# Hymba layer on one core: parts of queries and keys in turn by rows, three transfers a head, values in four groups

## The chip, the core and the metric

The kernel runs on one core of one Trainium2 chip. Its engines are TensorE (PE in the profile; its weight loads are PEld), VectorE (DVE), ScalarE (ACT), GpSimd (POOL) and SyncE (SP), which here only issues transfers; ScalarE issues some too. The metric is device time in microseconds. Three runs of the kernel before took 2397.44, 2400.09 and 2403.56 us; the median is 2400.09.

## What is computed

One decoder layer on 2048 tokens of width 1024, in float32. The part that matters here is mixer B, the dilated attention: 8 heads of 64 channels, each in three branches with (window, dilation) of (128, 1), (512, 4) and (2048, 16). In each branch the keys are gathered by stride, a query sees at most 129 of them, and a bias row by distance is added. The three outputs are then weighted by their softmax denominators:

```python
for window, dilation in DSA_PATTERN:
    o, lse = dilated_branch(q, k, v, rel_bias, window, dilation)
    outs.append(o); lses.append(lse)
w = jax.nn.softmax(jnp.stack(lses, axis=0), axis=0)
return jnp.sum(w[..., None] * jnp.stack(outs, axis=0), axis=0)
```

Ahead of it stands one projection of the normed input (`w_in`), beside it mixer A (chunked gated linear attention, GLA), and behind both the output projection, a squared-ReLU MLP and the last norm.

## The kernel before, in words

The kernel has three stages, one after the other: the projection (to about 553 us), the attention with GLA woven in (to about 955 us), and output projection and MLP. Products in float32 are made of parts: a value is split into `hi`, a rounded copy, and `lo`, the rest.

*Projection.* `finish` takes each finished block of the projection. For queries and keys it makes the two parts on ScalarE and VectorE and stores them from ScalarE's queue (L250) to DRAM tensors `qD` and `kD`, one pair of heads each, with shape [2, 128, S]: first all rows of one part, then all rows of the other. A head has 64 of the 128 rows.

*Attention.* `load_head` (L524 to 534) brings a head's queries and keys in, with three tiles of 128 partitions by 2048 columns. `qs` holds a query's one part in the upper 64 partitions and its other part in the lower 64. `k1` and `k2` hold one part of the keys each, in both halves. A score is then two matmuls, `qs` against `k1` and `qs` against `k2` (L631 and L633), each with a contraction over all 128 partitions, so the four products of parts are summed. Each tile takes two transfers of 64 partitions, six in all.

The work of a branch is cut into units, 160 in all: the branch with dilation 16 has four blocks of 128 queries a unit, the others two. Loop step k emits the transposes of unit k, the value products of unit k-2 and the scores of unit k+3 (`AHEAD`). A score step on VectorE (L643) adds the bias and takes the row's minimum, and ScalarE takes the exponential (L644); transposed probabilities go back through PSUM (L653, L660, L662), and the value products (L672) are copied to the branch's output `O` (L675). `at_unit(n, ...)` hangs a piece of work on the emission of unit n's scores: `load_head` 13 units ahead of a head's first unit, four pieces of `pack_q` on GpSimd (L585, which regroups the queries by stride) 4 units ahead.

When both heads of a pair are through a branch, `after` stores `O` of the two dilated branches to DRAM (`boD`, L743, issued three steps later) and loads the next pair's values for that branch (`load_v`): one transfer for the first and the third branch, sixteen of 64 KB for the second (L547). In the next pair's first units `combine_load` (L696) reads `boD` back in token order into `cmb`, in two halves of eight token tiles, two transfers each. `combine` opens with L707 and L708 on VectorE, which read `cmb`, weighs the branches (L709 to L718, VectorE) and sums them on GpSimd (L724, L726). For pair pr with first unit `first`, the first half's load hangs on unit first+1 and its steps on first+6 and on; the second half's on first+8 and first+13 and on. The pair's second head hangs its `load_head` on unit first+7.

What sets the final order is the scheduler: the emitted program is placed anew by a simulated timeline, engine by engine, so an instruction may stand earlier or later than where it was emitted. On each engine, and on SyncE's queue, instructions then run in that order. Each tile of the attention comes from one ring of 25 slots; a transfer into a slot waits until its earlier user is done.

## Time and profile before

| | |
|---|---|
| median of three runs | 2400.09 us |
| the profiled execution | 2398.99 us |
| its span, first to last instruction | 2397.2 us |
| PE busy | 2306.6 us (96%) |
| DVE, ACT, POOL busy | 1561.9, 1148.0, 583.3 us |
| mean granted clock of TensorE | 0.985 |
| head loads: `qs`, `k` | 16 and 32 transfers of 512 KB |

The page gives an engine's busy time as a share of the span. A row of a timeline has the start, the duration, engine and line, the operation with its tiles, and in brackets the idle time ahead of it with what ended it. SPq is SyncE's queue: its rows are issues, and their duration holds waits between them. A row of a table by stretches has the stretch, its length, then busy time and instruction count of PE, PEld, DVE, ACT and POOL, then the granted clock of TensorE (1.00 is full), the busy share of the DMA engines and the GB/s that they moved.

### The profile page before, as it was taken

Reading aid. Unit: us, or ns where it says so; the run is one execution under the profiler, and the core shown is the slowest. Engines: PE = TensorE matmul, PEld = TensorE weight load, DVE = VectorE, ACT = ScalarE, POOL = GpSimd, SP = SyncE. Lnnn points to the kernel's source line nnn. Section 1 sums busy time; section 2 is a strip of 40 time slices with the busy share of each in tenths; the row PEclk is TensorE's granted clock in tenths of the full one; section 3 lists DMA queues with packets and bytes.
Section 4 is the critical chain, followed back from the end, with each engine's and each line's share of the span. In section 5 each row is a group of like instructions: output and inputs, shape, how many; then the busy total and the mean of one; then the engine's idle time right before and its main releaser. Section 6 shows DMA issues by size and latency. Waiting matters only on the chain.

```text
span 2397.2 us, 35124 instructions
## 1 busy us (share of the span) xinstructions
PE 2306.6 (96%) x12648; PEld 1989.9 (83%) x12648; DVE 1561.9 (65%) x2879; ACT 1148.0 (48%) x2181; POOL 583.3 (24%) x551
## 2 busy tenths in 40 slices
PE   6999998999999989999999999999999999999998
PEld 5877898779989988888788887888888888888886
DVE  6878666765667668445677778877773455556555
ACT  5565434533767657223455556555563333224323
POOL 5555435446566665100000000000000100001002
PEclk9999999999999999999999999999999999999999
DMA  6457664757888867468664447544467496457653
GB/s 159 120 164 230 213 189 136 206 166 194 213 193 226 225 174 241 154 201 267 203 206 145 145 149 242 176 162 157 155 203 274 155 315 208 168 170 248 217 167 106
DMA packets 342540, 458.13 MB, mean 191 GB/s; under 512 B 19620, under 2 KB 215733, under 8 KB 336094
## 3 DMA queue, kind: packets, MB, share of 16 engines
q1 hardware_dynamic: 313614, 413.15, 56.0%
q10 hardware_dynamic: 28752, 42.74, 5.2%
q8 instruction: 99, 1.62, 0.3%
q14 instruction: 75, 0.61, 0.1%
HBM read 293.51 MB, written 167.02 MB: 192 GB/s over the span
## 4 chain that ended last, share of the span: by engine, by line
PE 77%; DMA 8%; DVE 7%; issue 3%; ACT 3%; POOL 1%; SPq 1%; ACTq 0%; POOLq 0%; DVEq 0%
PE ps_a L67 8%; PE ps_a L68 8%; PE ps_a L69 8%; PE ps_c L67 7%; PE ps_c L69 7%; PE ps_c L68 7%; PE ps_d L67 4%; PE ps_d L69 4%; PE ps_d L68 4%; PE ps_a L672 4%; PE ps_o L67 3%; PE ps_o L68 3%; PE ps_o L69 3%; PE ps_d L653 2%; DMA cmb<-boD 2%
## 5 line engine op out<-in xcount | busy, mean ns | idle before, releaser
L1226 POOL TENSOR_TENSOR suma<-suma,gs 128x512 f32<-128x512 f32 x16 | 23.3, 1472 | 1152.6 <-ACT scr L1224 1152.5
L346 DVE TENSOR_TENSOR ca<-ra,ca 128x1024 fp32r<-128x1024 f32 x112 | 137.7, 1230 | 164.4 <-ACT ca L345 164.4
L345 ACT ACTIVATE ca<-ra 128x1024 fp32r<-128x1024 f32 x112 | 118.0, 1054 | 225.8 <-PE ps_c L69 185.4
L345 ACT ACTIVATE w1comb<-w1raw 128x512 fp32r<-128x512 f32 x224 | 139.6, 627 | 158.7 <-PE ps_c L69 57.7
L644 ACT ACTIVATE pe<-pe,O 128x256 f32<-128x256 f32 (+1 forms) x384 | 157.6, 454 | 89.1 <-DVE O L643 76.3
L672 PE MATMUL ps_a<-v,pt 128*128 128x65 f32 x1200 | 185.1, 258 | 13.3 <-DVE pt L662 8.5
L672 PEld LDWEIGHTS ps_a<-v,pt 128*128 128x128 f32 x1200 | 180.9, 200 | 16.1 <-DVE pt L662 9.5
L346 DVE TENSOR_TENSOR w1comb<-w1raw,w1comb 128x512 fp32r<-128x512 f32 x224 | 153.6, 689 | 53.4 <-ACT w1comb L345 53.2
L653 PE MATMUL ps_d<-ident,pe 128*128 128x128 f32 x600 | 160.9, 284 | 0.0
L643 DVE CUSTOM_DVE_ANT_0 pe<-ps_c,nb 128x256 f32<-128x256 f32 (+1 forms) x384 | 126.6, 360 | 43.4 <-PE ps_d L653 20.6
L204 DVE TENSOR_TENSOR wcomb<-wraw,wcomb 128x512 fp32r<-128x512 f32 (+2 forms) x84 | 101.2, 1210 | 70.3 <-ACT wcomb L202 68.8
L202 ACT ACTIVATE wcomb<-wraw 128x512 fp32r<-128x512 f32 (+2 forms) x126 | 96.3, 773 | 103.7 <-PE ps_a L69 20.8
L345 ACT ACTIVATE cb<-rb 128x1024 fp32r<-128x1024 f32 x56 | 59.4, 1061 | 158.0 <-PE ps_o L68 108.1
L67 PE MATMUL ps_c<-hb,w1comb 128*128 128x512 f32 x336 | 132.2, 393 | 2.8 <-ACT hb L345 2.8
L68 PE MATMUL ps_c<-hb,w1comb 128*128 128x512 f32 x336 | 132.2, 393 | 1.6 <-DVE w1comb L346 1.6
L69 PE MATMUL ps_c<-hb,w1comb 128*128 128x512 f32 x336 | 131.8, 392 | 0.0
L67 PE MATMUL ps_c<-cb,ca 128*128 128x512 f32 x336 | 130.8, 389 | 0.0
L68 PE MATMUL ps_c<-cb,ca 128*128 128x512 f32 x336 | 130.8, 389 | 0.0
L69 PE MATMUL ps_c<-cb,ca 128*128 128x512 f32 x336 | 130.8, 389 | 0.0
L653 PEld LDWEIGHTS ps_d<-ident,pe 128*128 128x128 f32 x600 | 111.1, 190 | 0.4
L94 POOL TENSOR_TENSOR stats<-stats,mhalf 128x1 f32<-128x1 f32 (+1 forms) x64 | 46.4, 730 | 259.3 <-DVE stats L93 216.1
L346 DVE TENSOR_TENSOR cb<-rb,cb 128x1024 fp32r<-128x1024 f32 x56 | 68.2, 1221 | 62.5 <-ACT cb L345 62.3
(351 smaller groups left out, 7330.2 us busy)
## 6 DMA issues: line engine op xcount, KB each, us to landing
ra<-actD SPq DMA_DIRECT2D x56, 1024.0 KB, 6.8
actD<-acc SPq DMA_DIRECT2D x192, 256.0 KB, 2.3
rb<-w_ff SPq DMA_DIRECT2D x72, 512.0 KB, 4.8
w1raw<-w_ff SPq DMA_DIRECT2D x32, 1024.0 KB, 7.3
k<-kD SPq DMA_DIRECT2D x32, 512.0 KB, 11.5
rb<-hTD SPq DMA_DIRECT2D x14, 1024.0 KB, 5.9
wraw<-w_in SPq DMA_DIRECT2D x48, 256.0 KB, 3.4
boD<-O SPq DMA_DIRECT2D x8, 1056.0 KB, 6.2
```

Source lines behind the costliest of these rows:

```text
L67: T.matmul(out, sh, mh, start=first, stop=False)
L68: T.matmul(out, sl, mh, start=False, stop=False)
L69: T.matmul(out, sh, ml, start=False, stop=last)
L94: G.tensor_tensor(r2, r, mhalf[:, :n], op=OP.pow)
L202: A.activation(hi, src, AF.Copy, scale=sc)
L204: V.tensor_tensor(lo, src, hi.bitcast(F32), op=OP.subtract)
L345: A.activation(hi, src, AF.Copy)
L346: V.tensor_tensor(lo, src, hi.bitcast(F32), op=OP.subtract)
L643: V.tensor_tensor_reduce(p, s, bias, scale=1.0, scalar=BIG, op0=OP.add, op1=OP.min, accum_out=nm)
L644: A.activation(p, p, AF.Exp, bias=nm, scale=-1.0)
L653: T.transpose(pb[:, i * 128:i * 128 + 128], src, ident)
L672: T.matmul(self.b.opsum[:, n % 4], self.pt[:, i * 128:i * 128 + 128], self.b.v[:, blk, cols], start=first, stop=last)
```

## The change

Three things are changed. The DRAM tensors of query and key parts have the two parts in turn by rows, [128, 2, S]: row r of part 0, row r of part 1, row r+1 of part 0. A head's 64 rows then are 128 rows that follow each other, and `qs` comes in one transfer over 128 partitions, with a query channel's two parts in neighbouring partitions. `k1` and `k2` come in one transfer each, whose source reads each row twice (a step of 0) into the two neighbouring partitions. The sums of a score are the same.

`load_head` is a generator of three pieces, hung 13, 11 and 8 units ahead of the head's first unit instead of all on 13; each piece takes its slot when it is issued. The sixteen value transfers of the second branch are issued in four groups of four, on four units that follow each other, instead of at once; for the first pair they are still issued at once.

```diff
-    qD = [dram.tile([2, 128, S], F32, name=f"qD{p}") for p in range(4)]
-    kD = [dram.tile([2, 128, S], F32, name=f"kD{p}") for p in range(4)]
+    qD = [dram.tile([128, 2, S], F32, name=f"qD{p}") for p in range(4)]
+    kD = [dram.tile([128, 2, S], F32, name=f"kD{p}") for p in range(4)]
...
-                A.dma_start((qD if kind == "dq" else kD)[pr][part, :, tk], c[:, 512 - 512 * part:1024 - 512 * part])
+                A.dma_start((qD if kind == "dq" else kD)[pr][:, part, tk], c[:, 512 - 512 * part:1024 - 512 * part])
...
     def load_head(h):
         pr, hh = divmod(h, 2)
-        qs, k1, k2 = slot("qs", FR, S), slot("k1", FR, S), slot("k2", FR, S)
-        rows = slice(64 * hh, 64 * hh + 64)
-        halves = [slice(64 * dup, 64 * dup + 64) for dup in range(2)]
-        for dup, half in enumerate(halves):
-            SP.dma_start(qs[half].bitcast(F32), qD[pr][dup, rows])
-        for part, t in enumerate((k1, k2)):
-            for half in halves:
-                SP.dma_start(t[half].bitcast(F32), kD[pr][part, rows])
-        return qs, k1, k2
-
-    def load_v(pr, br):
+        t = pairs[h] = [slot("qs", FR, S)]
+        SP.dma_start(t[0].bitcast(F32), qD[pr][64 * hh:64 * hh + 64].rearrange("r d s -> (r d) s"))
+        yield
+        for part in range(2):
+            t.append(slot(f"k{part + 1}", FR, S))
+            rows = kD[pr][64 * hh:64 * hh + 64, part]
+            SP.dma_start(t[-1].bitcast(F32), bass.AP(tensor=rows.tensor, offset=rows.offset,
+                                                     ap=[[2 * S, 64], [0, 2], [1, S]]))
+            yield
+
+    def load_v(pr, br, later=lambda n, f, *args: f(*args)):
...
-            for n in range(NT):
-                SP.dma_start(v[:, n], w[n // 4, :, :, n % 4])
+            for b in range(4):
+                later(b, lambda b: [SP.dma_start(v[:, 4 * b + r], w[b, :, :, r]) for r in range(4)], b)
...
-    pairs, outs = {0: load_head(0)}, {}
+    pairs, outs = {}, {}
+    list(load_head(0))
...
-            vs[pr + 1, b.br] = load_v(pr + 1, b.br)
+            vs[pr + 1, b.br] = load_v(pr + 1, b.br, lambda n, *f: at_unit(clock[0] + AHEAD + 1 + n, *f))
...
-                at_unit(first - 13, lambda h: pairs.update({h: load_head(h)}), b.h)
+                pieces = load_head(b.h)
+                for n in (13, 11, 8):
+                    at_unit(first - n, lambda p: next(p), pieces)
```

## The prediction

> **What bounds the kernel now.** I read the page's first part and chain, then the 20 us stretches of the attention stage (about 583 to 955 us), then who waits for whom there, and last the instructions around each hole.

> ```profile
> span 2397.2 us, 35124 instructions
> PE 2306.6 (96%) x12648; PEld 1989.9 (83%) x12648; DVE 1561.9 (65%) x2879; ACT 1148.0 (48%) x2181; POOL 583.3 (24%) x551
> PE 77%; DMA 8%; DVE 7%; issue 3%; ACT 3%; POOL 1%; SPq 1%; ACTq 0%; POOLq 0%; DVEq 0%
> ```

> TensorE is the bound: it is busy for 96% of the span, and 90.6 us of idleness are all that better feeding can give. The DMA share of the chain, 8%, is where a transfer edit could reach it. The stretches show where that is (busy us and instructions of PE, PEld, DVE, ACT, POOL; granted clock; DMA share; GB/s):

> ```profile
> 600.00:620.00 20.00, 20.00 (x188) 19.90 (x188) 13.79 (x61) 14.37 (x40) 11.61 (x15) 1.00 1.04 215
> 680.00:700.00 20.00, 14.27 (x112) 13.81 (x111) 11.64 (x49) 8.93 (x23) 16.99 (x20) 0.83 1.04 258
> 780.00:800.00 20.00, 16.85 (x119) 16.37 (x119) 13.21 (x51) 10.58 (x29) 18.74 (x22) 0.74 0.60 167
> 860.00:880.00 20.00, 12.22 (x89) 11.85 (x88) 12.05 (x61) 8.19 (x22) 11.53 (x13) 0.74 0.92 253
> ```

> An undisturbed stretch has 188 matmuls; three stretches have 112, 119 and 89, and in them the granted clock fell too. One wait stands at the head of all three:

> ```profile
> DVE small L707 <- DMA cmb<-boD: 25.7, 6, 11.2
> ...
> 690.48 0.62 DVE L707 TENSOR_TENSOR small<-O,cmb 128x16 f32<-128x16 f32 x1 [7.07 <-DMA cmb<-boD]
> ...
> 692.43 0.69 PE L672 MATMUL ps_a<-v,pt 128*128 128x65 f32 x2 [5.73 <-DVE pt L662]
> ...
> 782.79 0.64 DVE L707 TENSOR_TENSOR small<-O,cmb 128x16 f32<-128x16 f32 x1 [4.49 <-DMA cmb<-boD]
> ...
> 784.61 0.69 PE L672 MATMUL ps_a<-v,pt 128*128 128x65 f32 x2 [2.15 <-ACT pt L660]
> ...
> 867.74 0.17 DVE L707 TENSOR_TENSOR small<-O,cmb 128x16 f32<-128x16 f32 x1 [11.20 <-DMA cmb<-boD]
> ...
> 868.73 0.55 PE L631 MATMUL ps_c<-k,qp 128*128 128x256 f32 x1 [7.78 <-DVE small L710]
> ```

> L707 opens a pair's `combine`. It waits on VectorE for a tile loaded back from DRAM; behind it VectorE's other work stands still, and then TensorE does. Why the tile is late, from SyncE's queue:

> ```profile
> 670.43 1.12 SPq L530 DMA_DIRECT2D qs<-qD  x2
> 671.60 2.62 SPq L533 DMA_DIRECT2D k<-kD  x4
> 674.27 6.71 SPq L696 DMA_DIRECT2D cmb<-boD  x2
> ...
> 832.74 2.92 SPq L547 DMA_DIRECT2D v<-vD  x2
> ...
> 838.84 14.32 SPq L547 DMA_DIRECT2D v<-vD  x14
> ...
> 855.38 1.17 SPq L743 DMA_DIRECT2D boD<-O  x1
> ...
> 861.76 0.36 SPq L696 DMA_DIRECT2D cmb<-boD  x1
> ```

> The first two holes: the six head transfers (3.15 MB) stand directly ahead of the two `cmb` loads. The third: SyncE issued the store to boD only at 855.38, behind all sixteen value loads, so the `cmb` load of the same rows could follow only at 861.76.

> What the holes cost, stretch by stretch after PE resumes:

> ```profile
> 663.00:678.50 15.50, 15.50 (x138) 15.40 (x137) 10.86 (x61) 11.27 (x37) 9.15 (x12) 1.00 0.59 143
> 692.50:695.80 3.30, 3.30 (x17) 3.30 (x18) 3.23 (x17) 2.49 (x8) 1.53 (x2) 0.50 1.16 310
> 784.60:794.80 10.20, 9.20 (x46) 8.90 (x47) 8.61 (x31) 5.76 (x18) 9.02 (x12) 0.50 0.62 190
> 868.70:873.30 4.60, 4.58 (x23) 4.51 (x24) 4.60 (x29) 3.21 (x10) 0.00 (x0) 0.50 1.19 294
> ```

> At full clock 138 matmuls took 15.5 us (8.9 per us). At half clock the three stretches did 17, 46 and 23, worth 1.9, 5.2 and 2.6 us: a loss of 1.4, 5.0 and 2.0 us. With the idle time (5.73, 2.15, 7.78) the three places cost 7.1, 7.2 and 9.8, together **24.1 us**.

> **The change part by part.** *Transfers over all partitions.* Six of 64 partitions become three of 128 partitions, 1 MB each. The rates (first row: a head load of before; the others: reloads of 1 MB in one transfer over 128 partitions with rows of 8 KB, the form of the new `qs` load):

> ```profile
> 672.00:687.00 15.00, 14.70 (x127) 14.24 (x126) 7.79 (x32) 9.26 (x27) 14.68 (x18) 1.00 1.00 219
> ...
> 274.00:278.00 4.00, 4.00 (x36) 4.00 (x35) 0.00 (x0) 0.00 (x0) 1.78 (x1) 1.00 0.98 384
> ...
> 1119.50:1123.50 4.00, 4.00 (x28) 3.51 (x27) 2.04 (x5) 2.26 (x5) 0.36 (x1) 1.00 0.92 378
> ```

> With the engines equally busy the old form moves 219 GB/s, the full form some 380. 3.15 MB then take 8.3 us instead of 14.4. By itself this is worth nothing, since most head loads are hidden; what counts is what stands behind them. The `k` loads read each row twice (a step of 0 in the source); no row shows that form. Its bounds are the two rates, 2.8 and 4.8 us per MB; I take 3.0, since the destination is the same as `qs`'s. [...]

> *Order.* In the built order of the changed kernel (the scheduler places instructions anew) the second half of a pair's combine now reads `qs`, `cmb`, `cmb`, `k1`, `k2`: only 1 MB stands ahead of `cmb`. But the scheduler also moves L707 forward. Counted in score steps (L643, of which there are 384), L707 stood 10, 9 and 4 steps behind its last-needed `cmb` issue at the three holes, and now stands 4, 7 and 4 behind it; at two places that had no hole it goes from 8 to 6 steps, and from 3 to 8. A step takes 0.87 to 0.89 us (two rows each in the count):

> ```profile
> 600.00:660.00 60.00, 23.91 (x138) 1.00 0.88 215
> 700.00:760.00 60.00, 22.50 (x135) 1.00 0.76 206
> ```

> and landings are (KB, median us from issue):

> ```profile
> boD<-O SPq DMA_DIRECT2D x8, 1056.0 KB, 6.2
> cmb<-boD SPq DMA_DIRECT2D x16, 528.0 KB, 6.4
> qs<-qD SPq DMA_DIRECT2D x16, 512.0 KB, 8.8
> rb<-hTD SPq DMA_DIRECT2D x14, 1024.0 KB, 5.9
> v<-vD SPq DMA_DIRECT2D x4, 1024.0 KB, 6.8
> ```

> Place by place, against a slack of PE behind a VectorE wait of 1.3 us (7.07 less 5.73) to 3.4 (11.20 less 7.78):
> - First hole: `qs` 3 us, then `cmb` 528 KB about 2 us, with 2 us from issue to first byte and from last byte to semaphore, so it lands some 7.5 us after `qs` is issued; L707 comes 5 steps, 4.4 us, behind it and copies stand between. Wait 1 to 3, left on PE **0 to 1**; I take 0.5.
> - Second hole: the same 7.5 us against 8 steps, 7.0 us. Left **0**.
> - Third hole: the boD store moves from behind the sixteenth value load to behind the tenth, and in the built order 8 steps (7.0 us) ahead of the `cmb` load of its rows, so its landing (6.2) is covered. `cmb` lands 6.4 after issue, L707 comes 4 steps (3.5 us) behind: wait 3, left on PE 0 to 1.7, I take 1, and with 7 chances in 10 a half-clock stretch as at 784 (5.0): **4.5**.
> - First half of pair 2 (before: wait 0.4): 6 steps are 5.3 us against 6.4: wait 1, left **0.5**. Second half of pair 3: a 1 MB value load (6.8) now stands right ahead of `cmb`; 8 steps are 7.0 us against about 9: wait 2, left **0.5**.
> - For one more half-clock stretch among these four, at 3 in 10: **1.5**.

> Together 7.5 remain of 24.1: a gain of **16.6**.

> Whether a hole of 2 us brings the half clock decides 5 of these 7.5 us. Here one of 2.15 us did (rows 784.61 and 784.60), so I charge it; that it stays out is rival 4.

> *Values in four groups.* The count stays at sixteen; spread over units, each issued for 0.6 us, they sit beside PE work. Uncovered, a late group would be a late `v`, but that is used a pair's worth of units later: 0. *Fewer DMAs.* 24 issues fewer on SyncE, 0.5 us each, spread over 400 us: 0 on the path. *Later `k2`.* Its slot now comes free later: for head 4 it is issued at step 159 instead of 148 for use at step 192, 29 us later, and for head 7 at 296 for use at 320, 21 us against 6 of transfer: hidden. Behind that wait on SyncE stand the gated-attention loads (from 148/152 to step 160; their reader stands at 172, 10 us later against a landing of 5): hidden; if that cover goes, each us late is one us on PE.

> *The projection stage.* Stores of q and k keep 128 rows of 2 KB, at twice the pitch: no row separates the pitch; 0, with 1 us either way. The first head is loaded inside it, and there a weight load stands behind `k`, ahead of an idle PE:

> ```profile
> 491.64 0.50 PE L67 MATMUL ps_a<-tb,wcomb 128*128 128x512 f32 x1 [2.12 <-ACT wcomb L202]
> ```

> Between 0 and 2.1 us of that can go; I take 1, as other waits lie between.

> **The sum.** 2398.99 (this execution: 2397.2 and 1.8 around it) less 16.6 less 1 is 2381.4. The execution lies 1.1 under the median of 2400.09, so against the median 2382.5: **2383**.

> **Rivals.**
> 1. *The hoisted L707 keeps paying.* All of L707's new places are 4 to 8 steps behind `cmb`, 3.5 to 7 us, against a median landing of 6.4. If three of the five leave a hole like that at 784 (2.15 and 5.0), 21.5 remain and 2.6 are gained, 3.6 with the projection: 2396. For it: the scheduler's hoist. Against it: the last combine's wait of 1.99 us left no hole in which L707 is the cause.

> ```profile
> 932.69 0.36 DVE L707 TENSOR_TENSOR small<-O,cmb 128x8 f32<-128x8 f32 x2 [1.99 <-DMA cmb<-boD]
> ```

> 2. *The doubled `k` rows stay at 219 GB/s.* `qs` alone is faster, `k` behind `cmb` only occupies queues: the value load of pair 3 and the gated-attention loads come 4 us later, 2 to 4 us on PE: 2386.
> 3. *Slower.* At all five places L707 catches a `cmb` that is still in transfer, each leaving 2.15 idle and 5.0 of half clock: 35.8 against 24.1, 12 us more: 2411. It decides from the point where `cmb` lands 3.5 us or more behind L707's place at four places, which would need queues ahead of it as full as the 219 GB/s row. Against it: only `qs` stands ahead.
> 4. *Short holes leave the clock alone.* The half clock follows only where PE was idle for 5 us or more, as at 686 and 860; at 784 the half clock would then have come from the thinned work before the hole. Of the residues 5.0 go (3.5 at the third hole, 1.5 at the others): 2378. [...]

> That nothing changes at the holes would need `cmb` to wait for something other than the queue; the rows at 670 to 674 speak against it.

> **How the numbers follow.** Forecast 0.52, rival 1 0.20, rival 2 0.08, rival 3 0.10, rival 4 0.10. A change under 0.3% (7.2 us) is about what this measurement cannot tell from none, so faster means under 2392.9. Faster: 0.50 of the forecast, 0.08 of rival 1, 0.07 of rival 2, all of rival 4: 0.75. Same: 0.02, 0.10 and 0.01: 0.13. Slower: 0.02 of rival 1 and rival 3: 0.12. The range: below, no residue and 2.1 at 491, 2374; above, rival 1 with 1 more for the pitch, 2397; rival 3 and some of rival 1, 0.15, lie above it.

> **What would show it.** In the new profile L707 (now L709) waits in sum for under 12 us instead of 25.7; PE has no hole over 4 us between 590 and 945; head transfers move over 350 GB/s and land in about 6 us. Wrong: a new hole behind a `k` or gated-attention load, or half-clock stretches at places that had none.

## The result, and the profile after

The changed kernel takes 2387.28 us (median of four runs, 2384.51 to 2389.83); the kernel before, run beside it, 2398.84 (2397.44 to 2403.56). The ratio is 0.9953, with a 95% interval of 0.9935 to 0.9971: 0.5% faster. The forecast was 2383 in a range of 2374 to 2397, so the sign and the range were right and the gain (11.6 us) was two thirds of the 17 foretold. The profiled execution took 2389.83 us, its partner of before 2398.99.

Lines of the changed kernel stand two further down in the attention: L707 is now L709, L643 is L645, L672 is L674. The page's first part and its chain, changed kernel:

```profile
span 2388.0 us, 35096 instructions
PE 2306.9 (97%) x12648; PEld 1988.7 (83%) x12648; DVE 1563.7 (65%) x2879; ACT 1147.0 (48%) x2181; POOL 582.9 (24%) x551
PE 73%; DVE 8%; DMA 7%; issue 5%; POOL 3%; ACT 3%; ACTq 0%; SPq 0%; POOLq 0%; DVEq 0%
```

TensorE is as busy as before (2306.9 against 2306.6 us) and idles 81.1 us instead of 90.6. Who waits for `cmb`; then the stretch of a head load and its two `cmb` loads, the 20 us stretches that had the holes, and a stretch ahead of the third place:

```profile
DVE small L709 <- DMA cmb<-boD: 11.1, 6, 5.0
```

```profile
672.00:687.00 15.00, 14.54 (x124) 13.78 (x123) 10.10 (x40) 9.26 (x28) 14.60 (x18) 1.00 1.02 335
680.00:700.00 20.00, 17.94 (x152) 16.66 (x151) 16.81 (x62) 12.69 (x34) 19.75 (x20) 1.00 0.73 239
780.00:800.00 20.00, 20.00 (x182) 19.74 (x181) 13.35 (x54) 13.86 (x39) 19.52 (x23) 0.99 0.41 148
840.00:860.00 20.00, 18.01 (x148) 17.70 (x147) 13.78 (x62) 11.58 (x37) 12.75 (x17) 0.91 0.99 312
860.00:880.00 20.00, 17.02 (x134) 16.41 (x133) 14.20 (x60) 12.10 (x36) 17.70 (x20) 0.91 0.12 34
```

L709's waits fell from 25.7 to 11.1 us (those of the next line, L710, rose from 0.5 to 3.5), the stretch of the head load moves 335 GB/s where it moved 219 (over 350 was foretold), and the three thin stretches (112, 119 and 89 matmuls) now have 152, 182 and 134. No hole reaches 4 us. From issue to landing `qs` takes 6.6 us in the median, as foretold (about 6), and `k` 8.9. But the stretch from 840, which had 175, has 148: holes have moved. All of them between 590 and 940 that are over 0.85 us, in the timeline of TensorE, with VectorE's row at the third place:

```profile
690.73 0.44 PE L674 MATMUL ps_a<-v,pt 128*128 128x65 f32 x2 [1.14 <-DVE pt L664]
...
776.87 0.58 PE L633 MATMUL ps_c<-k,qs 128*128 128x256 f32 x1 [2.06 <-DVE O L645]
...
843.00 0.18 DVE L709 TENSOR_TENSOR small<-O,cmb 128x16 f32<-128x16 f32 x1 [4.99 <-DMA cmb<-boD]
...
844.04 0.35 PE L794 MATMUL ps_o<-gla 128*128 128x130 f32 x1 [1.99 <-issue]
...
867.37 0.69 PE L794 MATMUL ps_o<-gla 128*128 128x130 f32 x4 [2.10 <-issue]
...
868.93 0.42 PE L674 MATMUL ps_a<-v,pt 128*128 128x65 f32 x1 [0.88 <-DVE pt L664]
...
933.12 0.44 PE L674 MATMUL ps_a<-v,pt 128*128 128x65 f32 x2 [2.68 <-DVE pt L664]
```

Behind the holes ending at 776.87, 844.04, 868.93 and 933.12 the clock was halved, each time for 3.4 us:

```profile
776.90:780.30 3.40, 3.40 (x17) 3.40 (x18) 2.44 (x12) 3.40 (x11) 3.40 (x4) 0.51 1.15 306
845.10:848.50 3.40, 3.40 (x20) 3.40 (x20) 2.54 (x20) 2.60 (x10) 1.48 (x3) 0.50 1.01 419
869.00:872.40 3.40, 3.40 (x19) 3.40 (x20) 2.58 (x17) 2.46 (x8) 2.00 (x2) 0.50 0.39 123
```

At the prediction's 8.9 matmuls per us, 17, 20 and 19 of them are worth 1.9, 2.2 and 2.1 us, a loss of 1.5, 1.2 and 1.3. So the places that cost 24.1 us now cost 1.1 (689), 3.6 (774), 3.2 (842) and 4.3 (865), together 12.2: a gain of 11.9. The hole at 774 is not mainly a wait for a transfer. L709 and L710 wait 0.97 and 0.33 us for `cmb` some 5 to 7 us ahead of it; what stands directly ahead, on VectorE and GpSimd, is this:

```profile
771.60 0.62 DVE L714 TENSOR_TENSOR small<-small,O 128x16 f32<-128x16 f32 x1
772.13 2.53 POOL L728 TENSOR_TENSOR O<-O,cmb 128x512 f32<-128x512 f32 x2
772.15 1.32 DVE L716 TENSOR_TENSOR small<-small,cmb 128x16 f32<-128x16 f32 x1
773.51 1.19 DVE L717 TENSOR_TENSOR small<-small 128x16 f32<-128x16 f32 x1
774.73 0.19 DVE L716 TENSOR_TENSOR small<-small,cmb 128x16 f32<-128x16 f32 x1
774.95 0.18 DVE L717 TENSOR_TENSOR small<-small 128x16 f32<-128x16 f32 x1
```

The same small steps of `combine`, L716 and L717 over 16 numbers a partition, take 0.19 us alone and 1.32 and 1.19 beside GpSimd's L728, which lasts until 774.66. The next score step of VectorE (L645), which TensorE waits for, stands behind them. This is the second cause that the experiments had to separate from the queue. For the holes ending at 844.04 and 867.37 the profile names no releaser ("issue"); in both, TensorE resumes 0.10 us after VectorE's L854 ends, so that they are VectorE's too is likely, not shown.

### The profile page after: what moved, and what is told of

Its sections match the earlier page's. It is cut to its first block, busy times and chain, and to the rows that moved or that the text cites. A ratio compares the mean times of both kernels' runs of the same rounds, so it can differ in the third digit from the quotient of the medians.

```text
span 2388.0 us, 35096 instructions
## 1 busy us (share of the span) xinstructions
PE 2306.9 (97%) x12648; PEld 1988.7 (83%) x12648; DVE 1563.7 (65%) x2879; ACT 1147.0 (48%) x2181; POOL 582.9 (24%) x551
## 4 chain that ended last, share of the span: by engine, by line
PE 73%; DVE 8%; DMA 7%; issue 5%; POOL 3%; ACT 3%; ACTq 0%; SPq 0%; POOLq 0%; DVEq 0%
PE ps_a L67 8%; PE ps_a L68 8%; PE ps_a L69 8%; PE ps_c L67 7%; PE ps_c L69 7%; PE ps_c L68 7%; PE ps_d L67 4%; PE ps_d L68 4%; PE ps_d L69 4%; PE ps_o L67 3%; PE ps_o L68 3%; PE ps_o L69 3%; PE ps_a L674 3%; PE ps_d L655 2%; PE ps_c L633 1%
## 5 line engine op out<-in xcount | busy, mean ns | idle before, releaser
L674 PE MATMUL ps_a<-v,pt 128*128 128x65 f32 x1200 | 183.1, 255 | 7.7 <-DVE pt L664 6.6
L674 PEld LDWEIGHTS ps_a<-v,pt 128*128 128x128 f32 x1200 | 178.8, 198 | 11.4 <-DVE pt L664 8.3
L645 DVE CUSTOM_DVE_ANT_0 pe<-ps_c,nb 128x256 f32<-128x256 f32 (+1 forms) x384 | 126.1, 361 | 39.5 <-PE ps_d L655 17.9
L202 ACT ACTIVATE wcomb<-wraw 128x512 fp32r<-128x512 f32 (+2 forms) x126 | 96.3, 773 | 110.0 <-PE ps_a L69 21.9
L67 PE MATMUL ps_c<-hb,w1comb 128*128 128x512 f32 x336 | 131.7, 392 | 2.4 <-ACT hb L345 2.4
L67 PE MATMUL ps_c<-cb,ca 128*128 128x512 f32 x336 | 130.8, 389 | 0.0
## 6 DMA issues: line engine op xcount, KB each, us to landing
ra<-actD SPq DMA_DIRECT2D x56, 1024.0 KB, 6.8
rb<-w_ff SPq DMA_DIRECT2D x72, 512.0 KB, 4.8
w1raw<-w_ff SPq DMA_DIRECT2D x32, 1024.0 KB, 7.6
k<-kD SPq DMA_DIRECT2D x16, 1024.0 KB, 8.9
rb<-hTD SPq DMA_DIRECT2D x14, 1024.0 KB, 5.7
boD<-O SPq DMA_DIRECT2D x8, 1056.0 KB, 4.5
```

The lines of the kernel that those rows point to most:

```text
L67: T.matmul(out, sh, mh, start=first, stop=False)
L202: A.activation(hi, src, AF.Copy, scale=sc)
L645: V.tensor_tensor_reduce(p, s, bias, scale=1.0, scalar=BIG, op0=OP.add, op1=OP.min, accum_out=nm)
L674: T.matmul(self.b.opsum[:, n % 4], self.pt[:, i * 128:i * 128 + 128], self.b.v[:, blk, cols], start=first, stop=last)
```

## The experiments

The kernel before was run again beside each set, with medians of 2395.77 (e1 to e4), 2394.74 (e5 to e8), 2395.82 (e9 to e11) and 2394.81 (e12); ratios are against those, and compare runs of different sets better than the times do.

| run | what | us | ratio (95%) |
|---|---|---|---|
| e1 | full transfers alone | 2382.07 | 0.9939 (0.9926 to 0.9953) |
| e2 | pieces alone | 2400.23 | 1.0013 (1.0003 to 1.0024) |
| e3 | value groups alone | 2398.62 | 1.0014 (1.0005 to 1.0023) |
| e4 | full transfers and pieces | 2393.23 | 0.9990 (0.9982 to 0.9999) |
| e5 | full transfers and groups | 2385.50 | 0.9958 (0.9946 to 0.9971) |
| e6 | changed kernel, VectorE's order by hand | 2419.97 | 1.0105 (1.0089 to 1.0122) |
| e7 | e1, VectorE's order by hand | 2419.53 | 1.0101 (1.0086 to 1.0116) |
| e8 | e1, `pack_q` on ScalarE | 2398.95 | 1.0018 (1.0007 to 1.0029) |
| e9 | e6 with little on GpSimd | 2383.05 | 0.9946 (0.9926 to 0.9965) |
| e10 | e1, store to boD earlier | 2382.07 | 0.9939 (0.9924 to 0.9954) |
| e11 | before, `cmb` ahead of the head | 2396.90 | 1.0001 (0.9988 to 1.0013) |
| e12 | e1, `cmb` ahead of the head | 2379.84 | 0.9938 (0.9924 to 0.9952) |

**e1 to e4: which part of the change does it.** e1 hangs all three pieces on 13 and issues the values at once (the line of the values is shown at e4):

```diff
-                for n in (13, 11, 8):
-                    at_unit(first - n, lambda p: next(p), pieces)
+                at_unit(first - 13, lambda p: list(p), pieces)
```

> Only the layout and the three full transfers of a head; all three are hung 13 units ahead, and the sixteen value transfers go at once. The built order on VectorE and on SyncE is that of before, but for the DMAs. Queue theory (the cmb tile was late because 3.15 MB at 219 GB/s stood ahead of it): the head now passes in about 8.3 us instead of 14.4, so cmb comes some 6 us earlier at the first two holes; L709's waits of 7.07 and 4.49 there fall under 2 and the holes of 5.73 and 2.15 us close. The third hole (7.78) has no head transfer ahead of it and stays. Gain 10 to 14: 2385 to 2389 against 2399 for before. Order theory (the gain comes from the pieces, which leave 1 MB ahead of cmb, and from the new order on VectorE; the rate counts little): the first two holes stay over 3 us in sum with waits over 4, 2395 to 2399.

e2 keeps layout and 64-partition transfers and takes only the pieces; e3 takes only the `later` argument of `load_v`; e4 is the changed kernel without it.

```diff
+        t = pairs[h] = [slot("qs", FR, S)]
+        for dup, half in enumerate(halves):
+            SP.dma_start(t[0][half].bitcast(F32), qD[pr][dup, rows])
+        yield
```

> Only the pieces: layout and six transfers of 64 partitions as before, two of them 13, two 11 and two 8 units ahead; values at once. Queue theory: ahead of cmb stands 1 MB at 219 GB/s, 4.8 us, instead of 3.15 MB in 14.4; but L709 stands only 4 steps behind its cmb instead of 10 at the first hole, so about 2 us of hole stay there, 1 at the second, and the third (store to boD behind sixteen values) stays: 2390 to 2394. Order theory: as good as the whole change, 2386 to 2389. If neither rate nor order but the value groups made the gain: 2397 to 2400.

> Only the value groups: head transfers as before. Queue theory: the store to boD leaves ahead of the last seven value loads, so the third hole (L707 waits 11.20, PE idle 7.78) shrinks to under 3 us, and the first two (5.73 and 2.15) stay as they were: gain 4 to 8, 2391 to 2395. If the third hole in the changed kernel closed for another reason than the groups (its head transfers being faster): 2397 to 2400 with the third hole over 5 us.

```diff
-            vs[pr + 1, b.br] = load_v(pr + 1, b.br, lambda n, *f: at_unit(clock[0] + AHEAD + 1 + n, *f))
+            vs[pr + 1, b.br] = load_v(pr + 1, b.br)
```

> The changed kernel with the sixteen value transfers at once. Queue theory: the store to boD stands behind all sixteen again, and a hole of 5 us or more opens at the third place (in the built order L709 comes 4 steps behind the cmb issue), 4 to 8 us more than the changed kernel's 2387: 2391 to 2395. The prediction's own sum counted the groups there with 5.3 us. If the groups do nothing: 2386 to 2389.

Of the four only e1 gains clearly (e4 by 0.1%), and as much as the whole change or more. Its timeline of VectorE and TensorE at the three places:

```profile
683.45 0.82 DVE L709 TENSOR_TENSOR small<-O,cmb 128x16 f32<-128x16 f32 x1 [0.23 <-DMA cmb<-boD]
...
689.72 0.39 PE L633 MATMUL ps_c<-k,qs 128*128 128x256 f32 x1 [1.13 <-DVE O L645]
...
773.37 0.25 DVE L709 TENSOR_TENSOR small<-O,cmb 128x16 f32<-128x16 f32 x1
...
780.17 0.44 PE L674 MATMUL ps_a<-v,pt 128*128 128x65 f32 x2 [1.30 <-DVE pt L664]
...
852.19 0.29 DVE L709 TENSOR_TENSOR small<-O,cmb 128x16 f32<-128x16 f32 x1 [5.61 <-DMA cmb<-boD]
...
854.03 0.55 PE L633 MATMUL ps_c<-k,qp 128*128 128x256 f32 x1 [3.04 <-DVE small L712]
```

With VectorE's order as before and the whole head still ahead of `cmb`, the waits of 7.07 and 4.49 us are 0.23 and nothing, and the holes of 5.73 and 2.15 are 1.13 and 1.30, at full clock. The head's three transfers run at 382 GB/s (672 to 681 us). So the first two holes were the queue's, and the faster head load was the remedy. (The DRAM layout and the number of transfers change with it; no run separates these from the rate.) The gain is 14 us on the medians, at the upper end of the queue theory's.

The third place was to stay as it was, and its hole went from 7.78 to 3.04. It does have a head load ahead, which prediction and forecast overlooked. SyncE's queue, the kernel before (directly ahead of the value loads at 832.74) and then e1:

```profile
830.27 1.64 SPq L533 DMA_DIRECT2D k<-kD  x2
```

```profile
820.21 0.55 SPq L534 DMA_DIRECT2D k<-kD  x1
...
822.86 15.17 SPq L549 DMA_DIRECT2D v<-vD  x14
...
840.25 0.39 SPq L745 DMA_DIRECT2D boD<-O  x1
```

Several of the value loads are issued just when a transfer of that head lands: before, at 835.11, 838.84 and 841.42, behind landings at 835.10, 838.82 and 841.40. So a faster head lets the sixteen values, and behind them the store to boD, go earlier: the store follows the last `k` issue by 20.0 us in e1 and by 24.1 before.

The pieces by themselves gain nothing (e2), and cost e1 11 us (e4). Much of that is one new place, in e4 at the turn to the output projection, VectorE's and TensorE's timeline:

```profile
954.28 2.36 DVE L726 TENSOR_TENSOR cmb<-cmb,small 128x512 f32<-128x512 f32 x2
956.56 2.36 DVE L728 TENSOR_TENSOR O<-O,cmb 128x512 f32<-128x512 f32 x2
958.83 0.68 DVE L346 TENSOR_TENSOR mT<-ps_d,mT 128x512 fp32r<-128x512 f32 x1
...
959.57 0.80 PE L68 MATMUL ps_a<-wo,mT 128*128 128x512 f32 x1 [6.41 <-DVE mT L346]
```

The scheduler put `mT`, TensorE's next operand, behind the last pair's sums. e2 has the same hole (6.44 us), and missed the queue theory's 2390 to 2394; the changed kernel and e1 do not have it. So e4's time lies where the queue theory had it, but for another reason: at the third place, where a hole of 5 us was foretold, it is 2.33. The groups are worth 5.9 us beside pieces and full transfers (2393.23 to 2387.28; by the ratios 0.37%, 8.9 us), and nothing beside the old transfers. That one hole, with half clock for 5.9 us behind it, is enough for the difference, so the groups' worth is a matter of the order that the scheduler happened to build, not of the store to boD. In e3 the third place was worse although the store went out earlier:

```profile
863.49 0.17 DVE L707 TENSOR_TENSOR small<-O,cmb 128x16 f32<-128x16 f32 x1 [12.27 <-DMA cmb<-boD]
...
865.23 0.55 PE L631 MATMUL ps_c<-k,qp 128*128 128x256 f32 x1 [9.42 <-DVE O L643]
```

L707 had moved from score step 302 to 296, and the wait grew; the queue theory's 2391 to 2395 missed.

**e5: full transfers and groups.** The changed kernel with all three pieces on 13, as in e1's diff.

> Full transfers, all three 13 units ahead, and the values in four groups: the changed kernel without its pieces. The groups cost the changed kernel nothing and saved 5.9 us there (2387.28 against 2393.23), but did nothing beside the old transfers. If what they do is to let the store to boD go earlier, the third place improves on the run with full transfers alone (there L709 waits 5.61 and PE idles 3.04 with a half-clock stretch): 2377 to 2381. If they act through the order on VectorE (L709 goes from score step 302 to 296, only 4 to 6 steps behind its cmb issues, as beside the old transfers, where it waited 12.27): 2382 to 2390, with a wait over 5 us there.

2385.50, 3.4 us over e1 (4.6 by the ratios, whose intervals overlap by a little): the order's branch. L709 waits 7.45 us at the third place, and the hole there is 4.60 (e1: 5.61 and 3.04). The changed kernel stands at the same ratio (0.9953 against 0.9958), so beside full transfers and groups the pieces make no difference that can be measured.

**e6, e7 and e9: the order by hand, and GpSimd.** e6 and e7 keep VectorE's instructions of the attention in emitted order, e6 in the changed kernel and e7 in e1:

```diff
-    for k in range(-AHEAD, NU + LAG):
...
+    with tc.manual_schedule(engines={nc.vector.engine}):
+        for k in range(-AHEAD, NU + LAG):
```

> The changed kernel with VectorE's attention instructions kept in the order in which they were emitted, so that L709 is not moved forward: it stands 14 to 17 steps behind the issue of its cmb in the first three pairs (4 to 8 in the changed kernel). Hoist theory (the residue comes from L709 placed too near its cmb): its waits fall from 11.1 us in sum to under 3, and of the residue at 689, 774, 842 and 865 (idle 1.14, 2.06, 1.99 and 2.10 us, three half-clock stretches) most goes: 2376 to 2382. Port theory (the residue comes from VectorE's small steps taking up to 1.3 us beside GpSimd, 0.17 alone): waits gone, yet holes of 1 to 2 us stay: 2383 to 2388. Rival: an order by hand puts score steps and copies behind others that are not ready, and TensorE waits elsewhere: over 2390.

> Full transfers alone (all 13 units ahead, values at once) with VectorE's attention instructions in the order as emitted; L709 stands 14 to 24 steps behind its cmb, but 0 to 14 at the second half of pair 0, whose cmb is issued at step 116 and read at 130. Against 2382.07 of full transfers alone: hoist theory: L709's wait of 5.61 at the third place and its hole of 3.04 go: 2374 to 2379. Port theory: 2379 to 2384. Rival, order by hand brings its own waits: over 2388.

Both are 1% slower than before, as the rival had it, and in neither does L709 wait for `cmb` at all. With the waits gone there are holes of 3.80, 5.66, 2.56, 4.59 and 6.53 us in e6, so holes do not need them; since the hand order also changes how the small steps stand, it does not price the hoist in the changed kernel. The hole ahead of 701.74, VectorE, GpSimd and TensorE, and one row of VectorE ahead of the hole of 4.59:

```profile
694.58 3.08 POOL L587 CAST qp<-qs 128x512 fp32r<-128x512 f32 x3
694.59 2.10 DVE L712 TENSOR_TENSOR small<-small,cmb 128x16 f32<-128x16 f32 x2
...
697.62 1.27 POOL L728 TENSOR_TENSOR O<-O,cmb 128x512 f32<-128x512 f32 x1
697.63 1.30 DVE L716 TENSOR_TENSOR small<-small,cmb 128x16 f32<-128x16 f32 x1
...
701.74 0.58 PE L633 MATMUL ps_c<-k,qs 128*128 128x256 f32 x1 [3.80 <-DVE O L645]
...
908.65 1.79 DVE L868 TENSOR_TENSOR wo<-woraw,wo 128x1024 fp32r<-128x1024 f32 x1 [7.32 <-ACT wo L867]
```

In emitted order the fourteen small steps stand in one piece, and beside GpSimd they last from 693 to 701. The holes of 5.66 and 2.56 stand behind such pieces too. Those of 4.59 and 6.53 do not: there VectorE waits 7.32 and 7.36 us for ScalarE's part of `wo`, an output weight, which the order by hand puts ahead of the scores. e9 leaves out most of GpSimd's work and keeps VectorE's order; its diff, in part:

```diff
-            qs = packed.get((h, br), qs)
...
+            if X is G:
+                rs = [r[:, :, :, :2] for r in rs]
```

> The changed kernel with VectorE's order by hand, as in the run of 2419.97, but with most of GpSimd's work left out: pack_q is left out (the scores take the unpacked queries) and the sums of combine (L726, L728) run over 2 of 64 channels, so the output is not the layer's. L709 waited 0.0 us in the run by hand, so its holes of 3.80, 5.66, 2.56, 4.59 and 6.53 us are not the queue's. Port theory: the small steps of combine (L709 to L720, means of 183 to 479 ns, sole ones 170) fall to about 170 to 200 ns each, the holes shrink under 1.5 us each, and with the half-clock stretches behind them 20 to 35 us go: 2385 to 2400. Order theory (the hand order itself is at fault: a chain of fourteen steps in one piece ahead of the scores): the holes stay over 2 us in the mean and 2408 to 2420.

e9 takes 2383.05, 37 us less than e6 and 2 less than the least foretold. Two groups of small steps by lines (busy us, mean ns of one, idle before), e6 and then e9, whose lines stand one further up:

```profile
L717 DVE TENSOR_TENSOR small<-small 128x16 f32<-128x16 f32 (+1 forms) x20 | 8.0, 398 | 0.7
L716 DVE TENSOR_TENSOR small<-small,cmb 128x16 f32<-128x16 f32 (+1 forms) x20 | 7.5, 374 | 0.3
```

```profile
L716 DVE TENSOR_TENSOR small<-small 128x16 f32<-128x16 f32 (+1 forms) x20 | 4.9, 244 | 0.7
L715 DVE TENSOR_TENSOR small<-small,cmb 128x16 f32<-128x16 f32 (+1 forms) x20 | 3.6, 178 | 0.3
```

The means fall from 398 to 244 and from 374 to 178 ns. The three holes behind the small steps go from 3.80, 5.66 and 2.56 us to 1.09, under 0.85 and 1.02. The piece ahead of the first of them takes 3.0 us in e9 (690.84 to 693.85), where in e6 it took 7.9 (693.05 to 700.99). Since the order is the same and no wait for `cmb` was there, these three holes are VectorE's small steps, which take longer beside GpSimd, as the expectation called port theory had it; that a port is behind it no run shows. (e9 also spares TensorE any wait for the packed queries, but no hole of e6 over 1 us was one.) The hole of 5.20 at 917 that e9 keeps is the wait for `wo` again:

```profile
920.00 1.23 DVE L869 TENSOR_TENSOR wo<-woraw,wo 128x1024 fp32r<-128x1024 f32 x1 [6.04 <-ACT wo L868]
```

**e8: the packed queries on ScalarE.**

```diff
-        G.tensor_copy(dst, src)
+        A.activation(dst, src, AF.Copy)
```

> Full transfers alone, with the 60 copies of pack_q (L587, 1.1 us each on GpSimd) on ScalarE. Port theory: VectorE's small steps of combine (L709 to L720, means of 157 to 557 ns by form) come nearer to 0.17 us, and the holes of 1.13, 0.73, 1.30 and 0.70 us at 688 to 784 shrink: 2377 to 2381 against 2382.07. Rival: ScalarE has 60 copies of about 0.6 us more between the exponentials, and the built order moves L709 forward at the later places (from 224 to 222, 302 to 296): 2383 to 2392, with the small steps no shorter in the mean.

2398.95: the rival's time, and worse. The small steps did get shorter, as the port theory had it (L709 to L720 from 351 to 262 ns in the mean, e1 and e8), but the copies take 1.1 us on ScalarE too, not 0.6, and TensorE now waits for ScalarE:

```profile
590.55 0.33 PE L655 MATMUL ps_d<-ident,pe 128*128 128x128 f32 x1 [3.79 <-ACT pe L646]
...
616.78 1.54 PE L674 MATMUL ps_a<-v,pt 128*128 128x65 f32 x6 [3.73 <-ACT pt L662]
```

**e10 to e12: what `cmb` waits for.** e10 issues the store to boD one step behind its branch instead of three; e11 and e12 hang the second half's load three units earlier, in the kernel before and in e1.

```diff
-            issue_later(3, dst.rearrange("(b p r) n -> p b (r n)", b=4, r=4),
+            issue_later(1, dst.rearrange("(b p r) n -> p b (r n)", b=4, r=4),
```

> Full transfers alone (2382.07), with the store to boD hung one step behind its branch instead of three: in the built order only the third place and the end change, where the store goes from score step 292 to 288, the second cmb issue from 298 to 294 and L709 from 302 to 300, six steps behind it instead of four. Queue theory: L709's wait of 5.61 there falls by 1.5 to 3 us, its hole of 3.04 under 1.5, perhaps with no half clock: 2377 to 2381. If the store's landing is bound by the value loads ahead of it and not by its issue: 2381 to 2384.

No gain: L709 waits 5.32 us there instead of 5.61 and the hole is 3.22 instead of 3.04. The store is issued 3.1 us earlier (837.11 against 840.25), and `cmb` 0.06 us behind the store's landing in both; but `cmb` then takes until 849.9, 7.4 us instead of 6.0, and L709 itself stands two steps earlier. Why this `cmb` is slower stays open.

```diff
-                        combine_at(pr - 1, 8 * half, 8, first - 2 + 7 * half, [first + 3 + 7 * half + n for n in range(6)])
+                        combine_at(pr - 1, 8 * half, 8, first - 2 + 4 * half, [first + 3 + 7 * half + n for n in range(6)])
```

> The kernel before with its 64-partition transfers; only the load of cmb for the second half of a combine is hung three units earlier, so that it stands ahead of the six head transfers in SyncE's queue at the first two places; VectorE's L707 moves forward too, to 2 or 3 steps behind the issue at the first and 4 at the second. Queue theory (what counts is what stands ahead of cmb, not the rate of the head): L707 waits 3 to 4 us instead of 7.07 at the first place, 2 to 3 instead of 4.49 at the second, the third is left as it is: gain 4 to 9, 2388 to 2394. If the rate counts (the head's packets share the DMA engines with cmb's whatever the order of issue): 2396 to 2402, with waits over 5 us.

> Full transfers alone, with the load of cmb for the second half hung three units earlier, so that it is issued ahead of qs, k1 and k2 as in the run with the old transfers (there the two cmb loads of the first place, issued ahead of six head transfers, landed 8.6 us after issue, and L708 waited 4.34 for the second of them). VectorE's L709 moves forward to 2 or 3 steps behind the issue. If the head's slow packets behind it were what held cmb up, it now lands within 6 us and L709 and L710 wait 2 to 3.5 us together at the first place; in all 2382 to 2388, since L709 stands nearer to cmb than in full transfers alone (2382.07). If any head behind it shares the DMA engines with cmb whatever its rate: landing over 7.5 us, waits over 4.5 us together, 2388 to 2396.

SyncE's issues and VectorE's waits at the first place, e11 and then e12:

```profile
671.48 1.05 SPq L696 DMA_DIRECT2D cmb<-boD  x2
672.57 1.78 SPq L530 DMA_DIRECT2D qs<-qD  x2
...
680.68 0.54 DVE L708 TENSOR_TENSOR small<-small,cmb 128x16 f32<-128x16 f32 x1 [4.34 <-DMA cmb<-boD]
```

```profile
665.29 1.05 SPq L698 DMA_DIRECT2D cmb<-boD  x2
666.38 1.19 SPq L529 DMA_DIRECT2D qs<-qD  x1
...
672.37 0.18 DVE L710 TENSOR_TENSOR small<-small,cmb 128x16 f32<-128x16 f32 x1 [2.18 <-DMA cmb<-boD]
```

In e11 the `cmb` loads are issued ahead of the head, and still the second was awaited until 680.68, 9.2 us after their issue began at 671.48; in e12, with full transfers behind, until 672.37, 7.1 us after 665.29. In the kernel before, two `cmb` loads at 657.21 with only two transfers of 256 KB behind them had landed after 6.5. So at these three places `cmb` came later with a head issued behind it, and latest with one in 64-partition transfers; what else was in flight at each was not compared. For e11 the time is the rate theory's (1.0001). Its first place is a little better than before (waits of 1.17 and 4.34 us on L707 and L708, a hole of 2.98 for 5.73), but its third has 8.10. e12's waits (0.92 and 2.18) are those foretold, its time is below the range; at 0.9938 it is not told apart from e1 and e10. These three have lower ratios than the changed kernel, but the intervals overlap (0.9924 to 0.9954 against 0.9935 to 0.9971): that leaving out pieces and groups is better is likely, not shown.

## Why the prediction was right, and where it was not

- *What bounds it, and the remedy.* Right, and shown: with nothing changed but layout and form of the head loads, the waits of the first two places go and their holes shrink to 1.1 and 1.3 us (e1). The doubled `k` rows, taken at 3.0 us per MB, run at the full rate: 382 GB/s over a head load in e1. Rival 2 falls.
- *Order: "only 1 MB stands ahead of `cmb`".* The step was wrong as a mechanism. What stands ahead does not decide (e1 has all three loads ahead and hardly a wait; e2 has one at the old rate, and L709 waits 2.69 and 3.57 us at the first two places), and with the head behind it `cmb` was still awaited until 9.2 us after its issue (e11). In the changed kernel the second `cmb` landed 10.0 us after `qs` was issued, not 7.5. What counts in these runs is the time that the whole head takes and how far behind the issue L709 stands: ten steps in e1.
- *First hole, 0.5 left.* 1.1, at full clock. L709 waited 0.79 us. The 2 us put there beside the transfers, from issue to first byte and from last byte to semaphore, stands there without a row: the 64 KB loads of `nb` landed 2.0 us after issue in the kernel before (median of 8), but a 1 MB load of `ra` with nothing else in flight (issued at 1884.78) had 1.0 us ahead of its first packet and 0.4 behind its last.
- *Second hole, 0 left.* 3.6 us. L709 waited 0.97, near enough; ahead of the hole stand VectorE's small steps beside GpSimd. The sum had no term for that, although in the prediction's own row at 690.48 L707 took 0.62 us over 16 numbers, and 0.17 at 867.74.
- *Third hole, 4.5 left.* 3.2 at 842: idle 1.99 instead of 1, half clock 1.2 instead of 3.5 (0.7 times 5.0). L709 waited 4.99 where 3 was put: `cmb` landed 4.7 us after its issue, not 6.4, but SyncE issued it only at 838.25, when L709 was already waiting. That head 7's loads hold up the value loads, and so the store, was not in the sum.
- *First half of pair 2, 0.5 left.* No hole, though L709 and L710 waited 2.41 and 1.95 us.
- *Second half of pair 3, 0.5 left.* 4.3 us at 865. L709 waited only 0.94 us, at 858.8, and L710 nothing; ahead of the hole stand VectorE's small steps, two of L712 at 862.40 with 1.34 us together. That they make the hole is argued from these rows alone.
- *Half clock at 5.0 us a time.* Too dear each, too seldom: three stretches among these places lost 1.2 to 1.5 us each, 4.0 in all, against 5.0 foretold. Rival 4 falls: behind holes of 2.06, 1.99 and 2.68 us the clock was 0.50 or 0.51 for 3.4 us, though not for the 10 us of 784.
- *The residue in sum.* 7.5 foretold, 12.2 measured. This is the miss of some 5 us. That the time came out no further off was in part luck: the same reasoning, without the groups, would have met the hole of 6.41 us at the turn to the output projection (e4), for which it had no term.
- *Projection, gain of 1.* The hole at 491 went from 2.12 to 1.87 us (2.12 to 2.24 in the four traces with the old layout, 1.87 to 1.90 in nine of the ten with the new). This execution reached its first score step at 584.95, 2.07 us later than before (582.88), having fallen behind at waits near 240 and 380 us. Stores in the new layout run from 147 us on, so the order of time does not clear the change; but over all traces that step starts at 581.42 to 583.62 with the old layout and at 578.48 to 584.95 with the new. It looks like scatter between executions.
- *Values in groups, 0.* The transfers are hidden, as said; but the order that they bring was worth 5.9 us in this kernel, by the hole that e4 has, and nothing or less elsewhere (e3, e5). Edits that only move issues are not free here, since the scheduler turns them into another order on VectorE.
- *Rival 1, the hoisted L707.* L709 does wait 11.1 us in sum, and it leaves a hole at the third place. Ahead of the others its waits are under 1 us, and VectorE's small steps take more; how the two share these holes no run separates. Rival 3 needed four catches of a transfer; there was one.

The sum of this execution: 11.9 gained at the places, 2.1 lost ahead of them, and 0.6 lost elsewhere, not followed up: 9.2 in all (2398.99 to 2389.83).

## What to carry to other kernels

A head load moved 219 GB/s over 64 partitions at a time and 382 over 128 (e1), and that took the first two holes to 1.13 and 1.30 us, where the order of the queue alone left one of 2.98 at the first place (e11): try all 128 partitions before the order. Count a scheduler's new order as part of the price of any edit, and test parts alone: here one of three parts carried the gain and the other two only shuffled the rest. Look for what an awaited transfer stands behind further back than the next rows: the third place waited for a head load twenty issues earlier. And look at how long the short instructions behind a wait take, not only at the wait.

## What the runs showed of the hardware

**VectorE beside GpSimd.** In the changed kernel's attention, of the small steps L712, L714, L716 and L717 that no GpSimd instruction overlaps, 28 in the record, none took over 0.19 us; beside GpSimd they took up to 1.32. VectorE's instructions that read `ps_c` or `ps_a` did not change: L645 took at most 0.43 us beside GpSimd and without it, L677 the same. In e6 a small step beside one GpSimd instruction of 1.27 us took about as long, 1.30 (697 us), and with most of GpSimd's work left out the means of two groups fell from 398 to 244 and from 374 to 178 ns (e9). Why the small steps are longer there, and L645 and L677 are not, no run shows.

**`cmb` with more issued behind it.** Two `cmb` loads of 528 KB were complete 6.5 us after their issue began with 0.5 MB behind them (kernel before, 657 us), and were awaited until 7.1 us after it with a head in full transfers behind them (e12) and until 9.2 with one in 64-partition transfers (e11). In e11 the landings kept the order of issue: 8.6 us after it in the median for `cmb`, 10.7 for `qs` and 13.9 for `k`, issued one behind the other from 671.48 on.
